# Up projection of a gated MLP: seven half-size products per 256 weight columns

## The chip, the cores and the metric

The kernel runs on one core of one Trainium2 chip. The metric is the device time of one execution in microseconds (us), taken as the median of several runs; the profile is one execution of the same program, recorded by the hardware profiler.

The engines are TensorE (PE in the profile, its weight loads PEld), VectorE (DVE), ScalarE (ACT), GpSimd (POOL) and SyncE (SP), which issues nearly all DMAs.

## The reference

The kernel computes one decoder layer for 512 positions of width 1024: a token-mixing sublayer (windowed attention, spatial gating, cross-attention, gates, an output projection, a layer norm), and after it the channel-mixing sublayer that is changed here:

```python
D_MODEL, SEQ, D_FF = 1024, 512, 2816
def conv_ffn_sublayer(x, w_ffn_up, conv_w, conv_b, w_ffn_down, ln_g, ln_b):
    a, bval = jnp.split(x @ w_ffn_up, 2, axis=-1)      # [512, 1024] @ [1024, 5632]
    a = lax.conv_general_dilated(a, ...) + conv_b      # causal, per channel, width 3
    y = (jax.nn.gelu(a) * bval) @ w_ffn_down           # [512, 2816] @ [2816, 1024]
    return layer_norm(ALPHA * x + y, ln_g, ln_b)
```

## The kernel before

All weights pass through one stream. A load of 1 MB is brought into a `raw` tile (`emit_load`, lines 108 to 117, three buffers). Each half of it, a unit of 1024 elements per partition, is split into two fp32r parts that TensorE multiplies: ScalarE writes the rounded part `wh` (line 133), VectorE the rest `wl = raw - wh` (line 134). There are four buffers each of `wh` and `wl`; `unit()` hands out the next pair and lets the splits run two units ahead. A product of two split operands is three matmuls (`mm3`, line 220): `wl` by the data's high part, `wh` by its low part, `wh` by its high part.

The input of the up projection is the normed stream, transposed and split: `hTh`, `hTl`, eight blocks of 128 model rows by 512 positions. The loop at line 914 takes the 22 blocks of 128 features one by one: 24 matmuls of 512 columns for the convolved half (`pa`), 24 for the other half (`pb`), each over all eight model blocks into a PSUM bank. Blocks 0 and 1 go ahead of the loop in 256-column halves (tiles `up`). `up_end` (line 895) then does the convolution (one ScalarE pass, line 897, two VectorE passes, lines 898 and 899, all three reading PSUM), the gelu (line 900), the gating with `pb` (line 901), and splits the gated product into `h2` (lines 223 and 225). The down projection (`project`, line 816; tiles `y`) uses all eight PSUM banks and 528 matmuls.

The order on each engine is set when the program is built: a scheduler lays out the instructions by its own timeline and each engine then runs its list strictly in that order. An instruction whose input is late holds up all behind it on its engine.

## Time and profile before

| what | us |
|---|---|
| median of 3 runs | 822.16 (822.1 to 822.8) |
| the profiled execution's span, first to last instruction | 820.5 |
| PE busy | 807.0 (98%) |
| DVE busy | 382.5 (47%) |
| ACT busy | 284.4 (35%) |
| POOL busy | 20.4 (2%) |

The page gives no other time of the profiled execution than its span. A busy time is the union of an engine's instructions; matmuls are pipelined, so their durations (389 ns for 512 columns) are longer than the distance from one start to the next, which the chain of work shows. [...]

### The profile page before, as it was taken

What the parts mean: (1) busy time and instruction counts of PE and PEld (TensorE: products, weight loads), DVE (VectorE), ACT (ScalarE), POOL (GpSimd) and SP (SyncE); (2) the same over time, 40 slices, a digit from 0 to 9 for tenths busy, and PEclk for the clock granted to TensorE, in tenths of its full rate; (3) what the DMA queues carried; (4) which work ended last, traced back from release to release, by engine and by line L of the source; (5) the groups of instructions that cost most, each with busy time, mean ns of one, the idle gap of its engine ahead of it and who ended that gap; (6) DMA issues with size and microseconds to landing.
All of it is one profiled execution on the core that took longest, in us unless ns stands there. A gap on an engine that the chain in (4) does not pass through costs nothing.

```text
span 820.5 us, 9700 instructions
## 1 busy us (share of the span) xinstructions
PE 807.0 (98%) x4051; PEld 675.0 (82%) x4051; DVE 382.5 (47%) x591; ACT 284.4 (35%) x433; POOL 20.4 (2%) x32
## 2 busy tenths in 40 slices
PE   7999999999999999999999999999999999999996
PEld 6878997778877788888888988888888888888884
DVE  4333235836664334335856455544454445225055
ACT  4331246665365222223611243333333333224000
POOL 2001000100000000000000000000000000000000
PEclk9999999999999999999999999999999999999998
DMA  9355331122402133242840023233333324224002
GB/s 317 124 196 182 103 129 52 52 78 82 150 26 78 52 103 128 78 152 89 323 154 1 1 103 102 103 103 103 103 103 102 103 83 131 94 102 154 1 26 77
DMA packets 62411, 87.10 MB, mean 106 GB/s; under 512 B 1994, under 2 KB 50154, under 8 KB 62368
## 3 DMA queue, kind: packets, MB, share of 16 engines
q1 hardware_dynamic: 60960, 82.32, 29.5%
q0 software_dynamic: 1408, 4.17, 1.5%
q8 instruction: 32, 0.52, 0.3%
q14 instruction: 11, 0.09, 0.0%
HBM read 84.36 MB, written 4.47 MB: 108 GB/s over the span
## 4 chain that ended last, share of the span: by engine, by line
PE 98%; DMA 1%; DVE 0%; SPq 0%; issue 0%; DVEq 0%
PE y L220 20%; PE gate L220 16%; PE pa L220 13%; PE pb L220 13%; PE qk L220 7%; PE zb L220 6%; PE proj L220 5%; PE v L220 4%; PE up L220 3%; PE oT L524 1%; PE sc L524 1%; PE qc L220 1%; PE pt L493 1%; PE qk L362 1%; PE vc L220 1%; PE kc L220 1%
## 5 line engine op out<-in xcount | busy, mean ns | idle before, releaser
L134 DVE TENSOR_TENSOR wl<-raw,wh 128x1024 fp32r<-128x1024 f32 (+1 forms) x127 | 154.1, 1214 | 186.5 <-ACT wh L133 177.7
L133 ACT ACTIVATE wh<-raw 128x1024 fp32r<-128x1024 f32 (+1 forms) x127 | 133.2, 1050 | 192.9 <-PE pb L220 47.2
L220 PE MATMUL y<-wh,h 128*128 128x512 f32 x256 | 79.0, 389 | 0.0
L220 PE MATMUL gate<-xTh,wl 128*128 128x512 f32 x192 | 76.7, 400 | 0.0
L220 PE MATMUL gate<-xTh,wh 128*128 128x512 f32 x192 | 75.0, 390 | 0.0
L220 PE MATMUL gate<-xTl,wh 128*128 128x512 f32 x192 | 74.9, 390 | 0.0
L220 PE MATMUL pa<-hTh,wl 128*128 128x512 f32 x160 | 62.3, 389 | 0.0
L220 PE MATMUL pa<-hTl,wh 128*128 128x512 f32 x160 | 62.3, 389 | 0.0
L220 PE MATMUL pa<-hTh,wh 128*128 128x512 f32 x160 | 62.2, 389 | 0.0
L220 PE MATMUL pb<-hTh,wl 128*128 128x512 f32 x160 | 62.2, 389 | 0.0
L220 PE MATMUL pb<-hTl,wh 128*128 128x512 f32 x160 | 62.2, 389 | 0.0
L220 PE MATMUL pb<-hTh,wh 128*128 128x512 f32 x160 | 62.2, 389 | 0.0
L220 PEld LDWEIGHTS y<-wh,h 128*128 128x128 f32 x256 | 48.0, 188 | 10.1
L220 PE MATMUL y<-wl,h 128*128 128x512 f32 x128 | 49.8, 389 | 0.0
L898 DVE SCALAR_TENSOR_TENSOR c<-pa,par,c 128x511 f32<-128x511 f32 x20 | 15.0, 750 | 65.8 <-ACT c L897 65.8
L220 PEld LDWEIGHTS gate<-xTh,wl 128*128 128x128 f32 x192 | 36.1, 188 | 8.6 <-issue 1.2
L220 PEld LDWEIGHTS gate<-xTh,wh 128*128 128x128 f32 x192 | 36.0, 188 | 7.8
L897 ACT ACTIVATE c<-pa,par 128x512 f32<-128x512 f32 x20 | 15.6, 781 | 76.1 <-PE pa L220 76.1
L220 PEld LDWEIGHTS gate<-xTl,wh 128*128 128x128 f32 x192 | 36.1, 188 | 7.0
L220 PE MATMUL qk<-xTh,wl 128*128 128x512 f32 (+1 forms) x96 | 35.8, 374 | 0.0
L220 PE MATMUL qk<-xTh,wh 128*128 128x512 f32 (+1 forms) x96 | 35.7, 371 | 0.0
L220 PE MATMUL qk<-xTl,wh 128*128 128x512 f32 (+1 forms) x96 | 35.6, 372 | 0.0
(219 smaller groups left out, 1480.8 us busy)
## 6 DMA issues: line engine op xcount, KB each, us to landing
raw<-in_w_ffn_up SPq DMA_DIRECT2D x22, 1024.0 KB, 4.9
raw<-in_w_in SPq DMA_DIRECT2D x13, 1024.0 KB, 5.0
raw<-in_w_gate SPq DMA_DIRECT2D x12, 1024.0 KB, 5.0
raw<-in_w_ffn_down SPq DMA_DIRECT2D x11, 1024.0 KB, 4.7
raw<-in_w_out SPq DMA_DIRECT2D x4, 1024.0 KB, 4.7
shear<-vecs POOLq DMA_DIRECT2D x1, 2304.0 KB, 14.1
raw<-in_w_mem_kv SPq DMA_DIRECT2D x2, 1024.0 KB, 5.3
raw<-in_w_proj_b SPq DMA_DIRECT2D x4, 512.0 KB, 3.3
```

The costliest lines, as they stand in the source:

```text
L133: nc.scalar.activation(h3, src, AF.Copy)
L134: nc.vector.tensor_tensor(l3, src, h3.bitcast(F32), op=ALU.subtract)
L220: nc.tensor.matmul(ps, w, v, start=first, stop=last)
L362: nc.tensor.matmul(ps[:, sl], w[a][:, k, :], xs(k0 + k, sl)[c], start=k0 + i + k == 0, stop=k0 > 0 and i == 2 and k == 3)
L493: nc.tensor.transpose(pt[:, kb, u, :], self.p[:, u, kb * P:(kb + 1) * P], ident)
L524: nc.tensor.matmul(ps, w, v, start=first, stop=last)
L897: nc.scalar.activation(c, pa, AF.Identity, bias=CB(i), scale=CW(2, i))
L898: nc.vector.scalar_tensor_tensor(c[:, 1:], pa[:, :S - 1], CW(1, i), c[:, 1:], op0=ALU.mult, op1=ALU.add)
```

## The change

Feature blocks 0 to 3 stay as they were. From block 4 on the loop takes two blocks, 256 weight columns, at a time, for each of the two halves of `w_ffn_up`. The 1024 x 256 weight is seen as 2 x 2 blocks (model rows by feature blocks), the data as 2 x 2 (model rows by 256 positions), and the product is formed from seven block products in place of eight (Winograd's form of Strassen's scheme): four of them use sums of weight blocks or data blocks. Each block product has four model blocks, so 12 matmuls of 256 columns.

The names: a `Seven` object holds one PSUM bank `xx`, whose left half collects four products one after the other, and one bank `yz` with two running sums. Between its products `xx` is copied out by ScalarE: to `cu` (lines 292 and 299) and `u3` (line 303). VectorE forms the outputs in the `ab` tiles (lines 296, 304, 310). Here the products are called x1, y, x2, z1, x3, x4 and z2, in the order of the code. x4 and z2 (`finish`) are issued after the next object's x1. GpSimd forms the weight sums (lines 125 to 127 and 151), GpSimd and VectorE once the data sums (`data_sums`). A load now gives four units: 1024, 1024 (the sums), 1024 and 512 elements. The gated product stays whole and is split during the down projection (`H2s`).

```diff
+    wsum = ctx.enter_context(tc.tile_pool(name="wsum", bufs=2))
-    work = ctx.enter_context(tc.tile_pool(name="work", bufs=6))
+    work = ctx.enter_context(tc.tile_pool(name="work", bufs=7))
...
     def emit_load():
...
+        if n in seven_loads:
+            s = wsum.tile([P, 2, 512], F32, tag="sums", name=f"sums{n}")
+            s2, s1 = [s[:, i, :].rearrange("p (k c) -> p k c", k=4) for i in range(2)]
+            a11, a21, a22 = v[:, 0:4, 0:P], v[:, 0:4, P:2 * P], v[:, 4:8, P:2 * P]
+            nc.gpsimd.tensor_tensor(s1, a21, a22, op=ALU.add)
+            nc.gpsimd.tensor_tensor(s2, s1, a11, op=ALU.subtract)
+            nc.gpsimd.tensor_tensor(a21, a11, a21, op=ALU.subtract)
+            sums[n] = s
...
     def emit_split():
...
+        if n in seven_loads and a == 8 and n not in halved:
+            halved.add(n)
+            a12 = raws[n][:, 4:8, 0:P]
+            nc.gpsimd.tensor_tensor(a12, a12, sums[n][:, 0, :].rearrange("p (k c) -> p k c", k=4),
+                                    op=ALU.subtract)
...
+    def seven_cols(src):
+        n = len(loads)
+        seven_loads.add(n)
+        add_load([P, 8, 256], src, [lambda r: r[:, :, 0:P], lambda r: sums[n],
+                                    lambda r: r[:, :, P:2 * P], lambda r: r[:, 4:8, 0:P]])
...
+    class Seven:
+        def __init__(self, raw, sums_, out1, out2, step=lambda: None):
...
+            xx, yz = bank("xx"), bank("yz")
+            self.x, self.y, self.z = xx[:, 0:256], yz[:, 0:256], yz[:, 256:512]
...
+        def p1(self):
+            self.u0 = unit()
+            self.product(self.x, self.part(self.u0, 0, False), self.raw, 0, 0)
+            nc.scalar.activation(self.cu[:, 0:256], self.x, AF.Copy)
+        def rest(self):
+            self.product(self.y, self.part(self.u0, 1, False), self.raw, 1, 0)
+            nc.vector.tensor_tensor(self.out1[:, 0:256], self.cu[:, 0:256], self.y, op=ALU.add)
+            u1 = unit()
+            self.product(self.x, self.part(u1, 0, True), self.sums, 1, 1, first=False)
+            nc.scalar.activation(self.cu[:, 256:512], self.x, AF.Copy)
+            self.product(self.z, self.part(u1, 1, True), self.sums, 0, 0)
+            self.u2, self.u3w = unit(), unit()
+            self.product(self.x, self.part(self.u2, 0, False), self.sums, 0, 1, first=False)
+            nc.scalar.activation(self.u3, self.x, AF.Copy)
+            nc.vector.tensor_tensor(self.out2[:, 256:512], self.u3, self.z, op=ALU.add)
+        def finish(self):
+            self.product(self.x, self.part(self.u2, 1, False), self.sums, 1, 0, first=False)
+            self.product(self.z, self.part(self.u3w, 0, False), self.raw, 1, 1, first=False)
+            nc.vector.tensor_tensor(self.out1[:, 256:512], self.cu[:, 256:512], self.z, op=ALU.add)
+            return self.x
...
+    def split_h2(j):
+        if j < NF // 2 and j not in h2s:
+            t = T8(f"h2s{j}", F32R)
+            s = 2 * j % 4
+            split_of(t[:, 0:2, :], t[:, 2:4, :], h2[j // 2][:, s:s + 2, :])
+            h2s[j] = t
...
-        nc.vector.tensor_tensor(c, c, pb, op=ALU.mult)
-        split_of(*H2(i), c)
+        return c
+    def up_end(i, pa, pb):
+        c = conv(i, pa)
+        nc.vector.tensor_tensor(H2(i), c, pb, op=ALU.mult)
...
-    for i in range(2, NF):
+    for i in range(2, UP8):
...
+        if i == 2:
+            hsums = data_sums(hTh, hTl, (nc.gpsimd, nc.vector))
...
+    def end_a(i, blk, outs):
+        first = blk.finish()
+        nc.scalar.activation(outs[1][:, t0], first, AF.Copy)
+        gated[i] = [conv(i + ii, outs[ii]) for ii in range(2)]
+    def end_b(i, blk, outs):
+        first = blk.finish()
+        c = gated.pop(i)
+        nc.vector.tensor_tensor(H2(i + 1)[:, t0], c[1][:, t0], first, op=ALU.mult)
+        nc.vector.tensor_tensor(H2(i + 1)[:, t1], c[1][:, t1], outs[1][:, t1], op=ALU.mult)
+        nc.vector.tensor_tensor(H2(i), c[0], outs[0], op=ALU.mult)
+    last = None
+    for i in range(UP8, NF, 2):
+        for end in (end_a, end_b):
+            outs = [W2("ab") for _ in range(2)]
+            blk = Seven((hTh, hTl), hsums, outs[0], outs[1])
+            blk.p1()
+            if last is not None:
+                last[0](*last[1:])
+            blk.rest()
+            last = (end, i, blk, outs)
```

`data_sums` adds four splits beside blocks 2 and 3, and each of the eleven calls of `split_h2` one, nearly all in the down projection; a split is one ScalarE and one VectorE instruction, here of 1024 elements per partition.

ScalarE in the old loop, one feature block and the start of the next (`c` is the convolution's tile):

```order
L897 ACTIVATE c_4593<-pa_4539,par_115 128x512 [waits PE_49]
L133 ACTIVATE wh97_4601<-raw56_4469 128x1024
L900 ACTIVATE c_4593<-c_4593 128x512 [waits DVE_49,Activation_49]
L133 ACTIVATE wh98_4632<-raw57_4500 128x1024 [waits PE_49]
L223 ACTIVATE h2_6_3534<-c_4593 128x512 [waits DVE_49]
L897 ACTIVATE c_4663<-pa_4607,par_115 128x512 [waits PE_49]
```

ScalarE in the new loop, from the third unit of a second object B (`xx_4538`, `cu_4540`) on; the first object of the pair, A, is `xx_4416`, and the next pair's is `xx_4668`:

```order
L144 ACTIVATE wh97_4542<-raw51_4294 128x1024 [waits DVE_49,PE_49]
L1057 ACTIVATE ab_4415<-xx_4416 128x256 [waits PE_49]
L144 ACTIVATE wh98_4614<-raw51_4294 128x512 [waits Pool_49]
L144 ACTIVATE wh99_4643<-raw52_4424 128x1024 [waits DMAHW1_49,PE_49]
L1021 ACTIVATE c_4591<-ab_4414,par_118 128x512 [waits DVE_49]
L1021 ACTIVATE c_4596<-ab_4415,par_118 128x512 [waits Activation_49]
L299 ACTIVATE cu_4540<-xx_4538 128x256 [waits PE_49]
L144 ACTIVATE wh100_4648<-sums52_4426 128x1024 [waits PE_49]
L1024 ACTIVATE c_4591<-c_4591 128x512 [waits DVE_49,Activation_49]
L1024 ACTIVATE c_4596<-c_4596 128x512 [waits DVE_49,Activation_49]
L303 ACTIVATE u3_4541<-xx_4538 128x256 [waits PE_49]
L292 ACTIVATE cu_4670<-xx_4668 128x256
```

The copies of `xx` now stand in one list with the splits and the convolution. The third unit's split (`wh97`) uses the buffer of A's third unit, which x3 and x4 of A read, and the next pair's first unit (`wh99`) stands three places behind it.

VectorE in the old loop, the same feature block:

```order
L898 SCALAR_TENSOR_TENSOR c_4593<-pa_4539,par_115,c_4593 128x511 [waits Activation_49]
L899 SCALAR_TENSOR_TENSOR c_4593<-pa_4539,par_115,c_4593 128x510 [waits DVE_49]
L134 TENSOR_TENSOR wl97_4602<-raw56_4469,wh97_4601 128x1024 [waits PE_49,Activation_49]
L901 TENSOR_TENSOR c_4593<-c_4593,pb_4568 128x512 [waits PE_49,Activation_49]
L134 TENSOR_TENSOR wl98_4633<-raw57_4500,wh98_4632 128x1024 [waits Activation_49]
L225 TENSOR_TENSOR h2_6_3534<-c_4593,h2_6_3534 128x512 [waits Activation_49]
```

VectorE in the new loop, the same place as ScalarE's list above:

```order
L145 TENSOR_TENSOR wl97_4543<-raw51_4294,wh97_4542 128x1024 [waits Activation_49]
L145 TENSOR_TENSOR wl98_4615<-raw51_4294,wh98_4614 128x512 [waits PE_49,Activation_49]
L310 TENSOR_TENSOR ab_4414<-cu_4418,yz_4417 128x256 [waits PE_49]
L296 TENSOR_TENSOR ab_4536<-cu_4540,yz_4539 128x256 [waits DVE_49]
L145 TENSOR_TENSOR wl99_4644<-raw52_4424,wh99_4643 128x1024 [waits DMAHW1_49,Activation_49]
L1022 SCALAR_TENSOR_TENSOR c_4591<-ab_4414,par_118,c_4591 128x511 [waits Activation_49]
L1022 SCALAR_TENSOR_TENSOR c_4596<-ab_4415,par_118,c_4596 128x511 [waits Activation_49]
L1023 SCALAR_TENSOR_TENSOR c_4591<-ab_4414,par_118,c_4591 128x510 [waits DVE_49]
L1023 SCALAR_TENSOR_TENSOR c_4596<-ab_4415,par_118,c_4596 128x510 [waits DVE_49]
L145 TENSOR_TENSOR wl100_4649<-sums52_4426,wh100_4648 128x1024 [waits Activation_49]
L304 TENSOR_TENSOR ab_4537<-u3_4541,yz_4539 128x256 [waits DVE_49,Activation_49]
L1064 TENSOR_TENSOR h2_2_4720<-c_4596,ab_4537 128x256 [waits DVE_49]
```

The convolution's passes (lines 1022 and 1023) now read `ab` tiles in SBUF in place of `pa` in PSUM, and the split of the next pair's first unit (`wl99`) stands behind two splits and two output sums.

ScalarE half a pair later, from the third unit of the next A (`xx_4668`) on, whose x2 is copied in the fourth row:

```order
L144 ACTIVATE wh101_4672<-raw52_4424 128x1024 [waits PE_49]
L144 ACTIVATE wh102_4737<-raw52_4424 128x512 [waits PE_49,Pool_49]
L144 ACTIVATE wh103_4766<-raw53_4546 128x1024 [waits DMAHW2_49,PE_49]
L299 ACTIVATE cu_4670<-xx_4668 128x256 [waits PE_49]
L144 ACTIVATE wh104_4771<-sums53_4548 128x1024 [waits DVE_49,PE_49]
```

The fourth unit's split (`wh102`) waits for B's z2, which read its buffer before, and the copy of x2 stands two splits behind it.

VectorE at the same place:

```order
L1063 TENSOR_TENSOR h2_2_4720<-c_4596,xx_4538 128x256 [waits PE_49]
L145 TENSOR_TENSOR wl102_4738<-raw52_4424,wh102_4737 128x512 [waits Activation_49]
L310 TENSOR_TENSOR ab_4536<-cu_4540,yz_4539 128x256 [waits PE_49]
L1065 TENSOR_TENSOR h2_2_4720<-c_4591,ab_4536 128x512 [waits DVE_49]
L145 TENSOR_TENSOR wl103_4767<-raw53_4546,wh103_4766 128x1024 [waits DMAHW2_49,Activation_49]
L145 TENSOR_TENSOR wl104_4772<-sums53_4548,wh104_4771 128x1024 [waits Activation_49]
```

The split of the second object's first unit (`wl103`) stands behind the half-size split, an output sum and the last gating product of the pair before.

On TensorE a steady pair (A and B) stands in this order, B' being the second object of the pair before: A.x1, seven matmuls of A.y, B'.x3, the other five of A.y, B'.x4, ten of A.x2, B'.z2, the other two of A.x2, A.z1, A.x3, B.x1, B.y, A.x4, A.z2, B.x2, B.z1.

## Rows read from the trace of the kernel before

**Rows 1.** The page: span, busy time of TensorE, and the chain's shares by engine.

```profile
span 820.5 us, 9700 instructions
PE 807.0 (98%) x4051; PEld 675.0 (82%) x4051; DVE 382.5 (47%) x591; ACT 284.4 (35%) x433; POOL 20.4 (2%) x32
PE 98%; DMA 1%; DVE 0%; SPq 0%; issue 0%; DVEq 0%
```

**Rows 2.** The chain in order of time: start us, us, engine, tile, line, matmuls.

```profile
497.21 5.44 PE pa L220 x24
693.05 119.69 PE y L220 x528
```

**Rows 3.** The same chain, stretches of 256-column matmuls.

```profile
205.77 5.76 PE vc L220 x48
461.04 14.39 PE up L220 x120
```

**Rows 4.** Groups of instructions on ScalarE, forms apart: xcount, busy us, mean ns, idle before.

```profile
L133 ACT ACTIVATE wh<-raw 128x1024 fp32r<-128x1024 f32 x125 | 131.9, 1056 | 188.0 <-PE pb L220 47.2 <-PE y L220 46.0 <-PE gate L220 34.3
L133 ACT ACTIVATE wh<-raw 128x512 fp32r<-128x512 f32 x2 | 1.3, 628 | 4.9 <-DMA raw<-in_w_in 4.9
L897 ACT ACTIVATE c<-pa,par 128x512 f32<-128x512 f32 x20 | 15.6, 781 | 76.1 <-PE pa L220 76.1
L223 ACT ACTIVATE kcT<-kc 128x256 fp32r<-128x256 f32 x2 | 0.8, 380 | 0.1
```

**Rows 5.** The same groups on VectorE.

```profile
L134 DVE TENSOR_TENSOR wl<-raw,wh 128x1024 fp32r<-128x1024 f32 x125 | 152.7, 1223 | 180.0 <-ACT wh L133 171.1 <-PE tm L677 8.6
L134 DVE TENSOR_TENSOR wl<-raw,wh 128x512 fp32r<-128x512 f32 x2 | 1.4, 687 | 6.6 <-ACT wh L133 6.6
L898 DVE SCALAR_TENSOR_TENSOR c<-pa,par,c 128x511 f32<-128x511 f32 x20 | 15.0, 750 | 65.8 <-ACT c L897 65.8
L225 DVE TENSOR_TENSOR kcT<-kc,kcT 128x256 fp32r<-128x256 f32 x2 | 0.8, 414 | 0.0
```

**Rows 6.** Instructions in order of time: start us, us, engine, line (steps and handoffs).

```profile
755.11 1.22 DVE L134 TENSOR_TENSOR wl<-raw,wh 128x1024 fp32r<-128x1024 f32 x1
756.25 1.22 DVE L225 TENSOR_TENSOR ll<-raw,lh 128x1024 fp32r<-128x1024 f32 x1
...
754.71 2.01 ACT L223 ACTIVATE lh<-raw 128x1024 fp32r<-128x1024 f32 x2
...
562.53 1.06 ACT L133 ACTIVATE wh<-raw 128x1024 fp32r<-128x1024 f32 x1 [2.36 <-PE pb L220]
563.62 1.23 DVE L134 TENSOR_TENSOR wl<-raw,wh 128x1024 fp32r<-128x1024 f32 x1 [0.34 <-ACT wh L133]
...
567.54 0.39 PE L220 MATMUL pa<-hTh,wh 128*128 128x512 f32 x1
567.77 0.39 PE L220 MATMUL pb<-hTh,wl 128*128 128x512 f32 x1
567.97 0.78 ACT L897 ACTIVATE c<-pa,par 128x512 f32<-128x512 f32 x1 [3.86 <-PE pa L220]
```

**Rows 7.** One tile's weight loads: duration ns min/median/max.

```profile
L220 PEld LDWEIGHTS pa<-hTh,wl x160: 188/188/192, 475.1 to 686.5; 128*128 128x128 f32 x160
```

**Rows 8.** Groups on GpSimd.

```profile
L649 POOL TENSOR_TENSOR mv<-mv,mhalf 128x1 f32<-128x1 f32 x12 | 11.2, 932 | 739.2 <-DVE mv L648 739.2
L248 POOL TENSOR_SCALAR_AFFINE_SELECT maskT<-maskT 128x128 f32<-128x128 f32 x1 | 0.3, 313 | 0.0
```

**Rows 9.** GpSimd and VectorE in order of time, last norm.

```profile
814.76 0.92 POOL L649 TENSOR_TENSOR mv<-mv,mhalf 128x1 f32<-128x1 f32 x1 [7.24 <-DVE mv L648]
814.53 1.41 DVE L851 SCALAR_TENSOR_TENSOR h<-h,mv,ln 128x512 f32<-128x512 f32 x2
815.86 1.41 DVE L855 SCALAR_TENSOR_TENSOR h<-h,mv,ln 128x512 f32<-128x512 f32 x2
```

**Rows 10.** DMA issues of the up weights: KB each, us to landing.

```profile
raw<-in_w_ffn_up SPq DMA_DIRECT2D x22, 1024.0 KB, 4.9
```

## The prediction

> **What bounds the kernel now.** I read the page first: TensorE is busy 807.0 of the 820.5 us span and makes 98% of the chain that ended last [rows 1]. Then the chain in order of time, which shows what a matmul really costs there: the 24 matmuls of a `pa` or `pb` group follow one another every 5.44 us, 0.2267 us each, with no gap from 497.21 to 693.05 us, where the down projection begins [rows 2]. So the stretch that the change rewrites, feature blocks 4 to 21, takes 693.05 - 497.21 = 195.84 us, which is 18 x 10.88, and nothing but TensorE sets it. All that VectorE and ScalarE do there is hidden. Last I read how long their instructions take and how quickly one engine follows another, since the new loop makes TensorE wait for them several times per pair of blocks.

> **The matmuls.** A pair of feature blocks needs 96 matmuls of 512 columns now, 21.76 us. It will need 2 x 7 x 12 = 168 of 256 columns. Stretches of such matmuls exist: 120 in 14.39 us and 48 in 5.76 us, 0.120 us each [rows 3], though one weight load lasts 0.188 us [rows 7], so that the loads overlap. One product of 12 takes 1.44 us, a pair 14 x 1.44 = 20.16 us. Over nine pairs that is 181.44 us, 14.4 less than now. This is all that the change can give; the rest is what it costs.

> **Busy time of the other engines per pair.** Back to back, VectorE starts a 1024-element split 1.14 us after the one before, 0.08 less than it lasts; ScalarE needs 2.01 - 1.06 = 0.95, say 0.96 [rows 6]. I take the same 0.08 to 0.10 off the others: VectorE 512 elements 0.61, a convolution pass 0.66, 256 elements 0.33 [rows 5]; ScalarE 512 elements 0.54, the first convolution pass 0.68, a 256-element copy 0.30 [rows 4]. ScalarE then has six full and two half splits, seven copies, four convolution passes (two at 0.54): 5.76 + 1.08 + 2.10 + 2.44 = 11.4 us. VectorE has 6 x 1.14 + 2 x 0.61 + 6 x 0.33 for the output sums, 4 x 0.66 and 0.33 + 0.33 + 0.61 for the gating: 13.95 us. Neither fills 20.16 us. What counts is the order of their lists.

> **First wait: the next pair's x1.** Count from the end of A.x4 on TensorE. It has 3 x 1.44 = 4.32 us of work left (A.z2, B.x2, B.z1) before the next pair's x1, whose weights come out of ScalarE's and VectorE's lists. A result is seen by ScalarE 0.20 us after the next matmul has started (567.77 to 567.97), and VectorE follows ScalarE at 0.03 (563.59 to 563.62) [rows 6]. ScalarE: `wh97`, whose buffer A.x4 has just freed, from 0.20, ends 1.26; copy of A.x4; `wh98`, ends 2.09; `wh99`, ends 3.06. VectorE: `wl97` 1.29 to 2.43, `wl98` to 3.04, two output sums to 3.70, `wl99` ends 4.92. That is 0.60 us late. How soon TensorE starts after VectorE has ended no row shows cleanly: between 0 and a weight load, 0.19 [rows 7]. I take the 0.03 of the only handoff of that kind. So 0.63 us.

> **Second wait: A.x3 and B.x1.** Count from the end of B'.z2, which frees the buffer of the half-size split. ScalarE: `wh102` from 0.20, ends 0.83; `wh103`, ends 1.80; only then the copy of A.x2, which has been ready since 0.44: it ends 2.08. A.x3 would start at 0.24 + 1.44 = 1.68. It waits 0.40 + 0.03 and ends at 3.55. VectorE: `wl102` 0.86 to 1.47, output sum to 1.80, gating product to 2.41, `wl103` ends 3.63, so B.x1 waits another 0.11. Together 0.54 us. Between the two waits B'.x4 needs the copy `u3` of B'.x3. Five matmuls of A.y, 0.60 us, cover 0.20 + 0.38 us: about 0.01 late. The sum is 0.63 + 0.54 + 0.01 = 1.18 us per pair, or 10.6 us in nine. With 0.19 in place of 0.03 at all four handoffs it would be 1.66.

> **What costs nothing.** The data sums run beside blocks 2 and 3, from 461.04 + 14.39 = 475.4 us [rows 3] to 497.2, and are first needed two products later, at about 500. In GpSimd's list the sum of weight load 47 stands before the last of them; that load waits for a buffer whose last split comes some three VectorE instructions into this stretch, near 479, and lands 4.9 us later [rows 10]. Two GpSimd operations (2.5 to 4 us) and two splits on each engine (5 us) follow, to about 493. Cover left: 7 us. In the loop a load is issued about a pair's length before its first use. The split of the gated product leaves the loop (two instructions per feature block) and comes back as 11 splits of 0.96 and 1.14 us in a down projection of 119.69 us [rows 2], where these engines have one split per 5.44 us. At the loop's end the first down-projection matmuls stand between B's last products and fill its waits. GpSimd's sums of a load are finished ahead of their split, unless VectorE blocks them (below).

> **The sum.** 195.84 - 181.44 - 10.6 = 3.8 us off the profiled execution's 820.5 us of span: 816.7. The runs' median lies 1.66 us above that span, 822.16; I keep that distance: **818.4 us**.

> **A cost the trace doesn't show: GpSimd beside VectorE.** Eight additions of 512 elements per pair go to an engine that did none. Its nearest rows are a select of 128 elements, 0.313 us, and a 128x1 power, 0.932 us [rows 8]. Per element the select would make an addition 1.25 us; VectorE does one in 0.69. I take 1.25, 10 us per pair. Does it slow VectorE? While the power ran (814.76 to 815.68), two VectorE passes with both operands in SBUF took 1.41 us, as did the next two without it [rows 9]. But that power reads two elements per partition, so the bound is from nothing to all. I take nothing as the likelier, by this row, and keep the other end as a rival. [...]

> **The rivals.**
> 1. [...] VectorE's instructions with two SBUF inputs take 8.06 (splits) + 2.64 (convolution) + 0.33 + 0.61 (gating) = 11.64 us per pair, GpSimd's 8 x 1.25 = 10. If they exclude each other the pair can't take less than 21.64 us, and since VectorE's list is in order, additions that started first delay `wl97` and `wl103` by half of one, 0.6 each, and the convolution in front of the `u3` copy by about 0.45. That is 21.34 + 1.65 = 23.0 at the far end; the middle, 22.3, gives 9 x (22.3 - 21.76) = +4.9: 827 us, range 821 to 833. It decides from 0.42 us of delay per pair. For it: the convolution now reads SBUF where it read PSUM, which makes every pass of it a candidate. Against it: rows 9.
> 2. Faster, all waits hidden. If TensorE's list, laid out with products between dependent ones, suffices, 14.4 us come off: 807.8. Against it stand the two list orders above; a chain shorter by 0.6 us would do.
> 3. The change doesn't do what it says: 168 matmuls need only 21.76 / 168 = 0.1295 us each to cost what 96 did. A weight load per 256 columns in place of 512 could do it, but 120 in a row at 0.120 speak against it: 822 to 825.

> **Chances.** A difference under 0.2% (1.6 us) can't be told from none here. Forecast 0.52, own range 815 to 822.5 (no handoff cost to 0.19 us each, and the late copies half a wait better); of it faster 0.44, same 0.08. Rival 1 0.30: same 0.09, slower 0.21. Rival 2 0.12, faster. Rival 3 0.06: same 0.02, slower 0.04. Faster 0.56, same 0.19, slower 0.25. The range leaves out the ends of rivals 1 and 2: 809 to 829.

> **What would show it.** Matmuls of the new form should start every 0.120 us inside a product and pairs repeat every 21.3 us. TensorE's idle time per pair should be two or three gaps: before an `xx` product waiting for the split `wl` of a first unit (0.6 and 0.1), and before an x3 waiting for ScalarE's copy (0.4). The 1024-element VectorE split should stay at 1.22 us and the down projection at 119.7 us. Splits or passes that lengthen, or start late with their input ready while GpSimd runs, mean rival 1; gaps under 0.2 us rival 2; a longer distance of matmuls rival 3. A longer down projection or a gap at block 4 would break a step that I cost at nothing.

## The result, and the profile after

The kernel after takes **831.5 us** (median of four runs, 829.0 to 832.4) against 822.2 us (822.1 to 822.8): a ratio of 1.0108, 95% interval 1.0096 to 1.0120. It is slower. The forecast was 818.4 us with a range of 809 to 829, so the sign and the range were both wrong.

The page of the profile after, its parts 1 and 4; they answer to [rows 1]:

```profile
span 829.4 us, 11339 instructions
PE 799.3 (96%) x4699; PEld 695.7 (84%) x4699; DVE 485.9 (59%) x686; ACT 337.0 (41%) x525; POOL 161.1 (19%) x109
PE 79%; DVE 14%; issue 3%; ACT 2%; DMA 1%; SPq 0%; DVEq 0%; ACTq 0%
```

TensorE made 98% of the chain before and makes 79% now; 14% is VectorE. TensorE's busy time fell by 7.7 us, yet the span grew by 8.9. The granted clock over the span was 0.997 before and is 0.996 now. The waits of TensorE in the new stretch, 497 to 712 us (columns: who waited for whom, us in total, times, longest):

```profile
PE yz L279 <- DVE ab L296: 8.2, 9, 2.2
PE xx L279 <- DVE wl L145: 4.5, 7, 1.7
PE xx L279 <- ACT cu L292: 1.6, 1, 1.6
PE xx L279 <- ACT u L303: 1.1, 1, 1.1
```

These are the waits that a view by releaser can see. Summed from one matmul's start to the next, less 0.120 or 0.2267 us each, TensorE loses 23.7 us there. A whole pair, from one B.x1 to the next, and a short stretch near the end, one engine's busy time after the other (length, TensorE, weight loads, VectorE, ScalarE, GpSimd, granted clock, DMA):

```profile
550.73:572.87 22.14, 21.03 (x168) 20.35 (x168) 19.16 (x22) 12.43 (x19) 14.21 (x8) 1.00 0.29 95
675.43:678.84 3.41, 3.41 (x19) 3.41 (x17) 3.41 (x5) 1.67 (x3) 1.35 (x1) 0.50 0.69 280
```

A pair has its 168 matmuls and needs 22.14 us in place of the 20.16 that 14 x 1.44 gives, at full clock. It is one of the shorter ones: seven pairs in a row take 21.5 to 23.3 us, 22.49 in the mean. In the second row the granted clock is 0.5, and 16 matmuls start 0.213 us apart in place of 0.120: 1.5 of the 23.7 us are not waits but this. Before it fell TensorE had waited 1.85 us at 664.23 and 2.38 us at 673.89.

What has grown is VectorE: 22 instructions of 19.2 us, where the prediction counted 13.95. Its groups in 497 to 700 us, which answer to [rows 5], and below them GpSimd's, which answer to [rows 8] (count, busy us, mean ns):

```profile
L145 DVE TENSOR_TENSOR wl<-raw,wh 128x1024 fp32r<-128x1024 f32 x37 | 55.8, 1507 | 27.6 <-ACT wh L144 27.5
L145 DVE TENSOR_TENSOR wl<-raw,wh 128x512 fp32r<-128x512 f32 x18 | 26.1, 1448 | 0.3
L1022 DVE SCALAR_TENSOR_TENSOR c<-ab,par,c 128x511 f32<-128x511 f32 x18 | 22.0, 1260 | 0.0
L145 DVE TENSOR_TENSOR wl<-sums,wh 128x1024 fp32r<-128x1024 f32 x17 | 21.0, 1237 | 2.7 <-ACT wh L144 2.7
L1023 DVE SCALAR_TENSOR_TENSOR c<-ab,par,c 128x510 f32<-128x510 f32 x18 | 12.6, 738 | 0.0
L1064 DVE TENSOR_TENSOR h<-c,ab 128x256 f32<-128x256 f32 x8 | 8.8, 1104 | 0.3
L296 DVE TENSOR_TENSOR ab<-cu,yz 128x256 f32<-128x256 f32 x18 | 7.4, 409 | 0.9 <-PE yz L279 0.9
...
L127 POOL TENSOR_TENSOR raw<-raw 128x512 f32<-128x512 f32 x17 | 36.5, 2148 | 0.0
L151 POOL TENSOR_TENSOR raw<-raw,sums 128x512 f32<-128x512 f32 x17 | 32.0, 1881 | 45.5 <-DVE wl L145 45.5
...
```

The half-size split went from 0.687 to 1.45 us, the 1024-element one from 1.22 to 1.51, a 511-element pass from 0.75 to 1.26. All of these read two tiles in SBUF. The output sum of line 296, whose second operand `yz` is in PSUM, still takes 0.41.

The means mix two cases. Of the 37 splits of `raw` with 1024 elements 17 begin while an addition runs and take 1.85 us in the mean; the other 20 take 1.22. Of the half-size splits 16 begin so, at 1.54, and two do not, at 0.69; of the 511-element passes nine, at 1.78, and nine not, at 0.74. No 510-element pass begins while an addition runs, and they stay at 0.74 us. The splits of the sums (`wl<-sums`) mostly start first or meet none; their mean is 1.24.

How that reaches TensorE, in one place: the timeline of VectorE, then GpSimd, then TensorE around the start of a second object B (start, duration in us):

```profile
565.33 1.35 DVE L1064 TENSOR_TENSOR h<-c,ab 128x256 f32<-128x256 f32 x1
...
566.93 1.98 DVE L145 TENSOR_TENSOR wl<-raw,wh 128x1024 fp32r<-128x1024 f32 x1
...
569.17 1.45 DVE L145 TENSOR_TENSOR wl<-raw,wh 128x512 fp32r<-128x512 f32 x1
...
571.60 1.22 DVE L145 TENSOR_TENSOR wl<-raw,wh 128x1024 fp32r<-128x1024 f32 x1
...
565.10 1.30 POOL L125 TENSOR_TENSOR sums<-raw 128x512 f32<-128x512 f32 x1 [3.14 <-DVE wl L145]
566.48 1.36 POOL L126 TENSOR_TENSOR sums<-sums,raw 128x512 f32<-128x512 f32 x1
567.79 2.28 POOL L127 TENSOR_TENSOR raw<-raw 128x512 f32<-128x512 f32 x1
...
572.05 0.28 PE L279 MATMUL xx<-th,wh 128*128 128x256 f32 x1
572.87 0.39 PE L279 MATMUL xx<-hTh,wl 128*128 128x256 f32 x1 [0.54 <-DVE wl L145]
```

Read it in steps. GpSimd's addition begins at 565.10; VectorE's gating product begins at 565.33 and ends at 566.68, 0.28 us after the addition's end; without additions it takes 0.42. GpSimd's next one runs from 566.48 to 567.84, so the split of 566.93 ends at 568.91. Now GpSimd's third, begun at 567.79, ends only at 570.07, 1.16 us after that split; so the half-size split of 569.17 ends at 570.62. Here the two engines take turns, each waiting for the other's whole instruction. The split that B.x1 needs starts at 571.60, though ScalarE's half of it was done at 570.32, and TensorE starts 0.05 us after its end, 0.70 us late.

The longest waits, those for line 296 before B.z1, come about in the same way. A little later in that pair (VectorE):

```profile
577.13 2.94 DVE L145 TENSOR_TENSOR wl<-raw,wh 128x1024 fp32r<-128x1024 f32 x2 [2.85 <-ACT wh L144]
```

These two splits, the second of half size, take 1.98 us in the kernel without additions (below). The output sum of line 296 stands behind them, ends at 580.73, and B.z1 starts at 580.78, 0.62 us late.

The same at the stretch's start, where the data sums run beside the first weight sums (VectorE, then GpSimd):

```profile
485.78 5.65 DVE L253 TENSOR_TENSOR tl<-tf,th 128x1024 fp32r<-128x1024 f32 x2
493.60 4.54 DVE L253 TENSOR_TENSOR tl<-tf,th 128x1024 fp32r<-128x1024 f32 x2
...
486.97 3.38 POOL L325 TENSOR_TENSOR tf<-tf 128x1024 f32<-128x1024 f32 x1
490.31 2.28 POOL L151 TENSOR_TENSOR raw<-raw,sums 128x512 f32<-128x512 f32 x1
```

Two such splits in a row take 2.35 us where GpSimd rests (in the kernel with all weight additions on VectorE, below); here they take 5.65 and 4.54. TensorE waits 1.75 us at 501.15 and 1.13 at 503.81, in the first pair. The kernel without additions (below) tells how much of that is due to the data sums.

### The profile page after: what moved, and what is told of

Read it like the earlier page. It is cut to its first block, busy times and chain, and to the rows that moved or that the text cites. A ratio compares the mean times of both kernels' runs of the same rounds, so it can differ in the third digit from the quotient of the medians.

```text
span 829.4 us, 11339 instructions
## 1 busy us (share of the span) xinstructions
PE 799.3 (96%) x4699; PEld 695.7 (84%) x4699; DVE 485.9 (59%) x686; ACT 337.0 (41%) x525; POOL 161.1 (19%) x109
## 4 chain that ended last, share of the span: by engine, by line
PE 79%; DVE 14%; issue 3%; ACT 2%; DMA 1%; SPq 0%; DVEq 0%; ACTq 0%
PE y L248 20%; PE gate L248 16%; PE qk L248 7%; DVE wl L145 7%; PE xx L279 6%; PE zb L248 6%; PE proj L248 5%; PE v L248 4%; PE yz L279 3%; DVE c L1022 2%; PE up L248 2%; PE oT L629 1%; PE sc L629 1%; PE qc L248 1%; PE pt L598 1%
## 5 line engine op out<-in xcount | busy, mean ns | idle before, releaser
L248 PE MATMUL y<-wh,h2s 128*128 128x512 f32 x256 | 79.5, 390 | 0.0
L279 PE MATMUL xx<-th,wl 128*128 128x256 f32 x216 | 62.5, 289 | 3.0 <-ACT cu L292 1.6
L279 PE MATMUL xx<-tl,wh 128*128 128x256 f32 x216 | 61.6, 285 | 0.0
L279 PE MATMUL xx<-th,wh 128*128 128x256 f32 x216 | 61.5, 285 | 0.0
L248 PEld LDWEIGHTS y<-wh,h2s 128*128 128x128 f32 x256 | 48.0, 188 | 10.2 <-DVE ab L310 0.3
L248 PE MATMUL y<-wl,h2s 128*128 128x512 f32 x128 | 49.8, 389 | 0.0
L279 PEld LDWEIGHTS xx<-th,wl 128*128 128x128 f32 x216 | 41.7, 193 | 4.4 <-ACT u L303 2.3
L279 PEld LDWEIGHTS xx<-tl,wh 128*128 128x128 f32 x216 | 41.9, 194 | 0.1
L279 PEld LDWEIGHTS xx<-th,wh 128*128 128x128 f32 x216 | 41.9, 194 | 0.0
L279 PE MATMUL yz<-hTl,wh 128*128 128x256 f32 x144 | 40.8, 283 | 0.0
```

The lines of the kernel that those rows point to most:

```text
L248: nc.tensor.matmul(ps, w, v, start=first, stop=last)
L279: nc.tensor.matmul(pp, ww(k), vv, start=first and k + i == 0, stop=k == 3 and i == 2, skip_group_check=not first)
```

## The experiments

All ratios are against the kernel before, run on the same chip, where it took 822.2 to 822.4 us. The first theory (A) is the prediction's rival 1: GpSimd and VectorE exclude each other. With the additions left out, left idle, and put on VectorE, it can be told from theory B, that the order of the lists costs more than was reckoned, and from theory C, that the splits wait for sums that come late.

**No additions.** The weight sums are left out; the second unit splits `raw` as it is. In the stretch the lists of TensorE, VectorE and ScalarE are, instruction for instruction, those of the kernel after.

```
-  nc.gpsimd.tensor_tensor(s1, a21, a22, op=ALU.add)      # and the three others
-  lambda r: sums[n],
+  lambda r: r[:, 0:4, :].rearrange("p (h a) c -> p h (a c)", h=2),
```

> The changed kernel without the four GpSimd additions per load; the second unit splits half of the raw weight in place of the sums, so the products are of other numbers (the sums are left out of the computation). The lists of ScalarE and VectorE in the loop stay as they are. Theory A (GpSimd additions and VectorE instructions with two SBUF inputs hold each other up): the 1024-element VectorE split falls back to 1.22 us in the loop, the TensorE gaps per pair fall from 2.6 us to between 1.2 and 1.7, time 816 to 821 us. Theory B (the order of the two lists and the handoffs cost more than I reckoned, GpSimd nothing): 829 to 832 us as the changed kernel.

Measured: 809.8 us, ratio 0.985 (0.983 to 0.986), below the range that theory A gave. Its VectorE group of the 1024-element split, a pair's busy times, with columns as above, and two splits of the data sums:

```profile
L139 DVE TENSOR_TENSOR wl<-raw,wh 128x1024 fp32r<-128x1024 f32 x58 | 70.8, 1224 | 36.4 <-ACT wh L138 36.0
...
553.20:573.50 20.30, 20.30 (x171) 20.22 (x169) 14.76 (x22) 12.48 (x20) 0.00 (x0) 1.00 0.32 107
...
486.02 4.57 DVE L246 TENSOR_TENSOR tl<-tf,th 128x1024 fp32r<-128x1024 f32 x2
```

The split is back at 1.22 us, the pair at 20.30, what TensorE loses in 497 to 710 us at 2.0. So the additions cost 831.5 - 809.8 = 21.7 us, which is the 23.7 - 2.0 us that TensorE loses less. It also shows that the waits of list order, 10.6 us in the prediction, come to 2.0 at most. And the data sums, made here by the same engines as in the kernel after, lengthen two splits to 4.57 us, yet TensorE has no gap at the start of the stretch: by themselves they cost nothing.

**Idle additions.** The same, with four GpSimd additions per load back, from `raw` into a scratch tile that nobody reads: the load without the dependency. The three lists in the stretch are again the same.

```
+  nc.gpsimd.tensor_tensor(s1, a11, a21, op=ALU.subtract)   # and the three others; the split still reads raw
```

> The same as the kernel without sums, but GpSimd does four additions per load again, of the same operands and size, into a scratch tile that nothing reads (the products are of other numbers again). No instruction of another engine waits for a sum. Theory A: VectorE splits lengthen to 1.4 to 2.2 us as in the changed kernel, time 828 to 832 us. Theory B: as the kernel without sums. Theory C (the units wait for late sums): also as the kernel without sums, 816 to 821 us.

Measured: 827.3 us, ratio 1.0056 (1.0041 to 1.0071), just below theory A's range. Its VectorE groups and the largest group of its waits:

```profile
L145 DVE TENSOR_TENSOR wl<-raw,wh 128x1024 fp32r<-128x1024 f32 x54 | 77.0, 1435 | 30.2 <-ACT wh L144 29.8
L145 DVE TENSOR_TENSOR wl<-raw,wh 128x512 fp32r<-128x512 f32 x18 | 25.7, 1428 | 0.1
...
PE yz L279 <- DVE ab L296: 7.5, 9, 1.3
```

Nobody waits for these sums, and still the splits lengthen to 1.43 us and 17.5 of the 21.7 us are back. The other 4.2 are left for sums that come late (theory C) and for the lower clock of the kernel after, which this profile does not show.

**Half of them on VectorE.** Two of the four additions move; the full computation.

```
-  nc.gpsimd.tensor_tensor(a21, a11, a21, op=ALU.subtract)
+  nc.vector.tensor_tensor(a21, a11, a21, op=ALU.subtract)   # and that of a12
```

> The full computation; of the four additions per load two stay on GpSimd and two go to VectorE, where 512 elements take 0.69 us against 1.27 us on GpSimd alone. Theory A: shared time per pair 11.64 + 4 x 0.66 + 4 x 1.25 = 19.3 us in place of 21.6, so less waiting: 821 to 828 us. Theory B: VectorE's list grows by 2.6 us per pair and GpSimd costs nothing, so slower than the changed kernel: 832 to 840 us.

Measured: 829.1 us, ratio 1.0083 (1.0068 to 1.0098); above what was expected. Two of its VectorE groups:

```profile
L145 DVE TENSOR_TENSOR wl<-raw,wh 128x1024 fp32r<-128x1024 f32 x37 | 58.5, 1582 | 5.3 <-ACT wh L144 5.0
L127 DVE TENSOR_TENSOR raw<-raw 128x512 f32<-128x512 f32 x16 | 12.3, 768 | 19.8 <-POOL sums L125 19.8
```

Half the additions did not mean half the cost: VectorE, which takes its list in order, now also waits 19.8 us for GpSimd's sum before its own; 5.1 us of TensorE's idle time stand at the start of the stretch alone. Behind that gap, from 501.6 us, the granted clock was 0.5 for 6.8 us, and from 607.4 for 3.4 us again (0.991 over the span), which is some 3.5 of the 21.8 us that TensorE loses. So this run doesn't give the price of two additions. The scheduler also moved ten of TensorE's matmuls per pair.

**All on VectorE.** The four additions as VectorE instructions; the full computation. The scheduler moves some ten matmuls per pair on TensorE, nearly as in the kernel before this one, which stayed at 829.1 us.

```
-  nc.gpsimd.tensor_tensor(...)    # all four
+  nc.vector.tensor_tensor(...)
```

> The full computation with all four additions per load on VectorE, none on GpSimd. VectorE then has 13.95 + 8 x 0.66 = 19.2 us of work per pair of 20.16. Theory A: no instruction lengthens any more, but the list in order is nearly full, so waits of 1.5 to 3 us per pair: 820 to 832 us. Theory B: VectorE's list alone decides and grows by 5.3 us per pair: 838 to 850 us.

Measured: 815.4 us, ratio 0.9918 (0.9903 to 0.9932): faster than the kernels before and after, and better than I had expected. The additions take 0.68 us each, the splits 1.22, a pair 20.41. The one large gap left is at the start (TensorE row):

```profile
501.94 0.38 PE L279 MATMUL xx<-th,wl 128*128 128x256 f32 x1 [2.49 <-ACT cu L292]
```

**Data sums on VectorE too**, and in a second kernel also asked for one step earlier; both the full computation. In the first the scheduler moves more of TensorE's matmuls; the second has the TensorE list of the kernel with only the weight additions on VectorE.

```
-  hsums = data_sums(hTh, hTl, (nc.gpsimd, nc.vector))
+  hsums = data_sums(hTh, hTl, (nc.vector, nc.vector))     # second kernel: ahead of up_end(0, ...)
```

> The kernel with all weight additions on VectorE, and the data sums on VectorE too (GpSimd then adds nothing in this stretch); the full computation. VectorE gets five more 1024-element instructions before the stretch (5 x 1.13 = 5.7 us) and loses the lengthening that GpSimd's three caused there (2.76, 1.55 and 2.76 us in place of 1.21, 0.69 and 1.21, 4.0 us). If the 2.6 us gap at the start of the stretch came from that lengthening and the handoffs between the two engines, it shrinks: 813 to 814.5. If it comes from VectorE's list being too full there, it stays or grows: 815 to 818.

> The same with the data sums asked for one step earlier, ahead of the gating of blocks 0 and 1; the full computation. If VectorE's list before the stretch is the limit, the earlier start takes the gap of 2.6 us away: 812 to 814. If the late gating of blocks 0 and 1 then holds PSUM banks and makes TensorE wait near 475 us, what is won at 500 is lost there: 815 to 818.

Measured: 813.2 us, ratio 0.9891 (0.9877 to 0.9906), and **812.2 us**, ratio 0.9879 (0.9865 to 0.9894), the fastest kernel with the full computation. The gap at the start shrinks to 0.4 + 0.6 us, then to nothing. In the second TensorE's listed waits come to 2.2 us. A pair of it:

```profile
558.42:578.83 20.41, 20.41 (x169) 20.21 (x169) 19.20 (x30) 12.43 (x19) 0.00 (x0) 1.00 0.32 104
```

VectorE is busy for 19.2 of a pair's 20.4 us, as long as in the kernel after, with 30 instructions in place of 22, and TensorE works through.

**What excludes what.** In place of the additions GpSimd writes zeros to the same places, or copies 512 elements to scratch; both leave the weight sums out.

```
+  nc.gpsimd.memset(s1, 0.0)          # first kernel, four per load
+  nc.gpsimd.tensor_copy(s1, a21)     # second kernel, four per load
```

> The kernel after, with each of GpSimd's four additions per load replaced by a write of zeros to the same 128x512 place: GpSimd still has four instructions per load in the same places of its list, but they read nothing. Left out: the weight sums, so the products with them multiply zeros. Theory A (what VectorE and GpSimd exclude each other over is reading SBUF): the 1024-element split is back at 1.22 us, the 512-element one at 0.69, pairs repeat every 20.3 us, and the time is that without the additions, 809 to 812. Rival (any GpSimd work on SBUF holds VectorE up): splits of 1.4 to 1.5 us as in the kernel with idle additions, 825 to 829.

> The kernel with idle additions, with each of GpSimd's four additions per load replaced by a copy of 128x512 into a scratch tile that nobody reads: it reads one operand where the addition read two. Left out: the weight sums. If every GpSimd instruction that reads SBUF excludes VectorE's two-input instructions, the copies lengthen them as the additions did: 1024-element splits of 1.35 us or more in the mean, 818 to 829 (less than the 827 of the additions where a copy is shorter). If only a GpSimd instruction with two inputs does, the splits stay at 1.22 and 0.69 us and the time is 809 to 812, that of the zeros.

Measured: 809.3 us, ratio 0.9845 (0.9831 to 0.9860), and 809.6 us, ratio 0.9845 (0.9829 to 0.9861). The two times alike would say that only additions collide, but the rows say more. Zeros (GpSimd, VectorE), then copies (GpSimd, VectorE):

```profile
575.64 0.53 POOL L127 MEMSET raw<- 128x512 f32 x1 [2.26 <-DMA raw<-in_w_ffn_up]
575.37 1.22 DVE L145 TENSOR_TENSOR wl<-sums,wh 128x1024 fp32r<-128x1024 f32 x1
```

```profile
575.74 1.42 POOL L125 COPY sums<-raw 128x512 f32<-128x512 f32 x1 [7.54 <-DMA raw<-in_w_ffn_up]
577.11 0.61 POOL L126 COPY sums<-raw 128x512 f32<-128x512 f32 x1
575.47 1.22 DVE L145 TENSOR_TENSOR wl<-raw,wh 128x1024 fp32r<-128x1024 f32 x1
```

A write inside a split: both keep their lengths, 0.53 and 1.22. A copy that starts inside a split lasts 1.42 in place of 0.61 and ends 0.47 us after it: it waited. So copies are held up too, seven in 61. Of 78 splits one was lengthened: here GpSimd, not VectorE, was nearly always the one that waited. That four copies take 2.5 us, where four additions take 5.1, is a likely reason, but it was not tested. My first alternative in the expectation was wrong in its time, and right in that a copy, too, excludes the split.

**The same additions in the kernel before**, from `raw` to scratch, from block 4 on; the full computation, TensorE's list unchanged.

```
+  if n in added:   # loads of blocks 4 to 21
+      nc.gpsimd.tensor_tensor(s1, a21, a22, op=ALU.add)      # and three others
```

> The kernel before, with the same four 512-element GpSimd additions per load of the up projection from block 4 on, into a scratch tile that nobody reads; the full computation. Theory A, and the view that only a TensorE which waits closely for VectorE pays for it: VectorE's splits of this stretch lengthen (mean 1.3 to 1.5 us in place of 1.22), but VectorE and GpSimd together need 4 x 1.14 + 2 x 0.61 + 10.2 = 16 us of the shared time in a pair's 21.76, TensorE's matmuls still follow each other without a gap, and the time is 821.5 to 824. If GpSimd's work costs by itself, whoever waits (its reads beside TensorE's, its place beside the DMAs), the time rises as it did after: 827 or more.

Measured: 822.3 us against 822.4, ratio 1.0001 (0.9991 to 1.0010). Its VectorE groups in 497 to 693 us, and a stretch of GpSimd and VectorE:

```profile
L142 DVE TENSOR_TENSOR wl<-raw,wh 128x1024 fp32r<-128x1024 f32 x36 | 49.9, 1386 | 6.1 <-ACT wh L141 6.1
L239 DVE TENSOR_TENSOR h<-c,h 128x512 fp32r<-128x512 f32 x18 | 19.9, 1108 | 0.0
L912 DVE SCALAR_TENSOR_TENSOR c<-pa,par,c 128x511 f32<-128x511 f32 x18 | 13.5, 750 | 52.6 <-ACT c L911 52.6
...
546.58 1.30 POOL L124 TENSOR_TENSOR sums<-raw 128x512 f32<-128x512 f32 x1
547.96 1.30 POOL L148 TENSOR_TENSOR sums<-raw,sums 128x512 f32<-128x512 f32 x1
...
547.07 0.75 DVE L912 SCALAR_TENSOR_TENSOR c<-pa,par,c 128x511 f32<-128x511 f32 x1 [3.33 <-ACT c L911]
548.53 1.81 DVE L142 TENSOR_TENSOR wl<-raw,wh 128x1024 fp32r<-128x1024 f32 x1
```

The splits lengthen as they did after (1.39 and 1.11 us), TensorE has no gap, and the time is the same. In this kernel, where TensorE does not wait closely for VectorE, the contention costs nothing (822.3 us against 822.4); and GpSimd's reads by themselves did not slow TensorE. The pass that reads `pa` in PSUM runs beside an addition, and neither gets longer: 0.75 and 1.30 us.

**Three split buffers**, on the kernel without additions: meant as a test of when a split may start.

```
-  wspl = ctx.enter_context(tc.tile_pool(name="wspl", bufs=4))
+  wspl = ctx.enter_context(tc.tile_pool(name="wspl", bufs=3))
```

> The kernel without additions, with three buffers in place of four for the split weights, so that a split has to wait for a later product than now. Left out: the weight sums. Theory: the prediction's waits of 1.18 us per pair were too large because it let each of the critical splits start only when one product more had ended than they really wait for; then a buffer fewer brings waits of that kind, 0.5 to 2 us per pair, and the time is 815 to 828. Rival: the handoffs have slack whenever the splits start, and TensorE's list covers a later start too: 809.5 to 812.

Measured: 829.0 us, ratio 1.0081 (1.0066 to 1.0096), a little above the theory's range. But the wait is another one:

```profile
PE xx L272 <- ACT u L296: 8.1, 17, 0.5
```

With three buffers the scheduler puts x4 directly behind x3, with nothing between for the copy of x3, and TensorE loses 0.63 us per object to that; 9.6 us more went before the stretch, which starts at 506.39 in place of 496.77. It doesn't decide the question that it was made for.

## Why the prediction was wrong

1. **The step that failed**: "I take nothing as the likelier, by this row, and keep the other end as a rival." The cost of GpSimd beside VectorE was 2.19 us per pair (22.49 - 20.30) over seven pairs, 3.1 us before them and 3.3 behind, 1.5 of these by the lower clock. Together that is the 21.7 us between 809.8 and 831.5. The row that I leaned on [rows 9] couldn't carry it: that power reads two elements per partition, an addition here reads 1024, and the prediction itself called the bound "from nothing to all". Why the power held nobody up was not tried. What the runs showed is this: a split of 0.69 us took 1.45 where both engines read two tiles in SBUF; one of 1.22 kept its length beside a write; a pass of 0.75 kept it with an operand in PSUM; and a GpSimd copy of 0.61 that began inside a split took 1.42. The prediction had no row of a GpSimd instruction of this size beside VectorE, so "nothing" was an estimate from that one weak row, and its cost stood in a rival alone.

2. **A term mis-sized**: the waits of list order, "1.18 us per pair, or 10.6 us in nine". Without additions they are 2.0 us in all. The count's start was wrong: "`wh97`, whose buffer A.x4 has just freed", and the half-size split counted from the end of B'.z2. ScalarE in the kernel without additions, the same places of a pair:

```profile
559.28 0.63 ACT L138 ACTIVATE wh<-raw 128x512 fp32r<-128x512 f32 x1 [0.51 <-PE xx L272]
561.92 1.06 ACT L138 ACTIVATE wh<-raw 128x1024 fp32r<-128x1024 f32 x1 [2.01 <-PE yz L272]
567.94 1.06 ACT L138 ACTIVATE wh<-raw 128x1024 fp32r<-128x1024 f32 x1 [1.06 <-PE yz L272]
569.38 0.38 ACT L1050 ACTIVATE ab<-xx 128x256 f32<-128x256 f32 x1 [0.38 <-PE xx L272]
```

The last row is the copy of A.x4, which starts when that product has ended. The split in question starts 1.44 us earlier, at the end of the y product before it: the pool gave it the buffer that came free first, not the one that is next by rotation. Likewise the half-size split runs at 559.28 behind x4, and only the 1024-element one at 561.92 waits for z2. So the split that the next pair's x1 needs ends at 573.14, 0.36 before x1, in place of 0.60 after. I had taken the rotation of four for granted, and the section on the change says the same of these buffers.

3. **A term put at nothing that held only by itself**: the data sums, with 7 us of cover. Alone they cost nothing, as the kernel without additions shows. Beside the first weight sums they do not fit: GpSimd's 1024-element operations took 2.4 to 3.4 us, the splits beside GpSimd's work about twice their length, and TensorE waited 1.75 + 1.13 us. With only the weight sums on VectorE a gap of 2.49 us remained there; with all of it on VectorE and earlier, nothing.

4. **What held**: the matmuls (0.120 us each, a product of 12 in 1.44, so rival 3 falls); a GpSimd addition priced at 1.25 us, measured at 1.27 to 1.30 where nothing meets it; the split of the gated product in the down projection, which loses 0.3 us in all. The places of the gaps did not hold. Of the prediction's four, B.x1 (0.11 us) has waits of 0.41 to 1.85 us and B'.x4 (0.01) four of 0.26 to 1.29; the next pair's x1 (0.63) and A.x3 (0.43) have none. The largest, before B.z1, 0.62 to 2.38 us, were not in it.

5. **The rivals**: rival 1 supposed the exclusion, which no row had shown, and gave 827 us, but as a sum of two errors that offset each other: 1.18 us per pair of waits, of which 0.14 came (20.30 - 20.16), and 0.96 of contention where 2.19 came. That its time came so near was luck. Rival 2, all waits hidden, is what the kernel does without the additions: 809.8 against 807.8.

## What to carry to other kernels

In these runs an elementwise operation given to GpSimd was not off VectorE's books where both read two tiles in SBUF: a 512-element addition kept VectorE's two-input instructions off while it ran, 1.3 us, twice the 0.61 to 0.68 that VectorE needed to do it itself. Writes and short copies cost nothing (809.3 and 809.6 us against 809.8), and VectorE instructions that read PSUM kept their length beside an addition (0.41 and 0.75 us); give GpSimd such work, and look first at whether anything waits closely for VectorE: in the kernel before, the same additions cost nothing (822.3 us against 822.4). When counting waits on buffers of a pool, look up which buffer each tile got, since a scheduler need not rotate them.
